# Block pairs of a fused matmul and rotary embedding, cut into two half-row tiles with mirrored weights

## The chip, the cores and the metric

The kernel runs on one core of a Trainium2 chip. The time is the device time of one execution in microseconds, as the profiler and the timer see it, and the kernels compared read the same inputs. Five engines work side by side: TensorE (PE, whose weight loads are listed apart as PEld), VectorE (DVE), ScalarE (ACT), GpSimd (POOL) and SyncE (SP). SyncE computes nothing and only issues transfers. Sixteen DMA engines move data between HBM and SBUF.

## The reference

The inputs are x (16 batches of 512 rows of 768 numbers), a weight of 768 x 768, and cos and sin of 512 x 64, all float32.

```
y = np.matmul(x, weight)                      # 8192 x 768 rows in all
y = y.reshape(batch, seq, 12, 64)
y1, y2 = y[..., :32], y[..., 32:]
out1 = y1 * cos1 - y2 * sin1                  # cos, sin by position in the sequence,
out2 = y2 * cos2 + y1 * sin2                  # the same for all heads and batches
out = np.concatenate([out1, out2], axis=-1)
```

## The kernel before, in words

The 8192 rows are cut into 64 tiles of 128 rows, and four tiles make a group, so there are 16 groups, g = 0 to 15. A group's result is 4 x 768 = 3072 columns of float32, which fill six of the eight PSUM banks: the tensor `py`. Two tiles make a pair, `(g, 0)` and `(g, 1)`; a pair owns three of the six banks.

TensorE contracts over partitions, so every tile of x must stand with its 768 inner numbers on partitions. There are two ways to that. An **ordinary tile** is loaded by SP as 128 rows of 3 KB into `xs` (`load`, L205), rounded to float16 by ACT into `xc` (`cast`), turned by TensorE through the identity into the PSUM tile `pt` (`turn_rows`, L266, twelve matmuls of 64 columns), and brought back to SBUF as `xt` by ACT. A **block pair** does without TensorE: four "quarters" of 32 partitions each are loaded so that each quarter holds a part of the inner dimension (`load_quarter`, L220), and one VectorE instruction turns 32 x 32 blocks for both tiles of the pair at once into `xp` (`turn_pair`, L294). Of the ten block pairs of the kernel before, `(g, 1)` for g = 5 to 14, the five with odd g are loaded in float32 by SP into `xb` and rounded by ACT into `xd` (`cast_pair`); the five with even g are loaded by a GpSimd DMA that rounds on the way, into `xh`.

The weight comes in six loads of 128 rows of 3 KB (`load_w`, L227), one for each of six chunks (t, e) of the inner dimension: inner number 6p + 2t + e stands on partition p. VectorE rounds each chunk to float16 as it comes (`cast_w`, `w_sb`). The first group starts with the chunks as they land (`mm0`, L334). From group 1 to 14 the matmuls are cut into two row halves: `walk` yields, for partitions 0 to 63 (r = 0) and 64 to 127 (r = 1), matmuls of 64 rows by 128 columns against 512 or 256 weight columns, and `both` interleaves the two streams so that the upper one is 1024 columns ahead of the lower (`LAG`). The two halves of a result add up in PSUM: one half opens a bank, and the other half closes it behind a wait on the PE's own counter (`one`, L359, `closed`).

When a bank is closed, VectorE multiplies it by cos and by sin into a product buffer (`rope`, L411, 1024 or 2048 products in one instruction), GpSimd adds the two products into the output tile `ov` (L428, one instruction of 1536 elements for a pair), and a DMA stores two tiles at a time (L449, 768 KB). There are three product buffers for groups 1 to 14, and one of them is the memory of the raw weight.

The order of the work is fixed when the program is written out. `do` records every instruction on its engine's queue with the semaphore waits that its buffers need; each engine runs its queue in order. The loop over tiles i = 4 to 63 emits matmuls for the tile, then `bturns` (the VectorE block turns, four tiles ahead), `turns` (about three ahead), `casts` (about five ahead), the GpSimd loads, and the stores. SP's loads stand in the list `fetch`; `pump` issues them as far as the ten `xs` and three `xb` buffers allow. The SP list begins with tiles 0 and 1 and weight chunk 0, tile 2 and chunks 1 and 2, tile 3 and chunks 3, 4 and 5, then cos, sin and tile 4.

Of the kernel before, what the change touches and what calls it, by code (L numbers as in the profile page):

```python
# [10 lines left out]
FP32 = mybir.dt.float32  # L11
FP16 = mybir.dt.float16
# [93 lines left out]
def kernel(  # L106
# [11 lines left out]
    f = Flow(nc, tc)  # L118
    do = f.do
    P = nc.NUM_PARTITIONS  # L120

    B, S, H = x.shape
# [3 lines left out]
    R = 32  # L126
# [3 lines left out]
    QB = 4  # L130
# [4 lines left out]


    BLOCKS = {}
    for g in range(5, 15):
        BLOCKS[g, 1] = "pool" if g % 2 == 0 and g >= 4 else "sp"

    def sbuf(name, shape, dt):
        return nc.alloc_sbuf_tensor(name, shape, dt).ap()

    NX, NB, NBH, NC, NCP, NXT, NXP, NOV = 10, 3, 3, 5, 2, 8, 4, 4

    ident = sbuf("ident", [P, P], FP16)
    cold = sbuf("cold", [P, 512], FP16)
# [6 lines left out]
    xh_b = [sbuf(f"xh{i}", [P, 2 * H], FP16) for i in range(NBH)]  # L154
# [23 lines left out]
    def ring(name, n, state={}):  # L178
        k = state.get((id(f), name), 0)
        state[id(f), name] = k + 1  # L180
        return k % n

    def copy(e, o, i_):
        return lambda eng: (
            eng.copy(out=o, in_=i_) if e == "act" else eng.tensor_copy(out=o, in_=i_)  # L185
        )

    def where(i):
        g, s = divmod(i, QB)
        return QB * (g // SB) + s, g % SB  # L190

    def pair_of(i):
        return i // QB, (i % QB) // 2
# [13 lines left out]
            writes=[f"xs{k}"], dma=f"xs{k}")  # L207

    def load_quarter(gh, q):
        g, h = gh  # L210
        b, r = where(g * QB + 2 * h)
        e = BLOCKS[gh]
        src = x[b : b + 2].rearrange("b (j a r) (q k) -> r q a (b j) k", r=SB, a=R, q=NQ)
        if q == 0:
            xs[gh] = ring("xh", NBH) if e == "pool" else ring("xb", NB)
        k = xs[gh]
        name = f"xh{k}" if e == "pool" else f"xb{k}"
        buf = xh_b[k] if e == "pool" else xb_b[k]
        dst = buf.rearrange("p (j k) -> p j k", j=2 * NQ)
        do(e, lambda eng: eng.dma_start(out=dst[ts(q, R)], in_=src[r, q]),  # L220
           writes=[f"{name}q{q}"], dma=name)

    wv = weight.rearrange("(p t e) n -> t e p n", t=NT, e=2)

    def load_w(c, e="sp"):
        t, h = c
# [9 lines left out]
    def cast(i, e):  # L236
        k = xs[i]
        c = ring("xc", NC)
        xc[i] = c
        do(e, copy(e, xc_b[c].rearrange("p (t m e) -> p t m e", t=NT, e=2),  # L240
                   xs_b[k].rearrange("p (m t e) -> p t m e", t=NT, e=2)),
           reads=[f"xs{k}"], writes=[f"xc{c}"])

    def turn(i, e):
# [29 lines left out]
    def cast_pair(gh, e="act"):  # L274
        k = xs[gh]
        c = ring("xd", NCP)
        xc[gh] = c
        do(e, copy(e, xd_b[c].rearrange("p (t j e) -> p t j e", t=NT, e=2),
                   xb_b[k].rearrange("p (j t e) -> p t j e", t=NT, e=2)),
           reads=[f"xb{k}q{q}" for q in range(NQ)], writes=[f"xd{c}"])  # L280

    def turn_pair(gh):
        g, h = gh
        z = ring("xp", NXP)
        dst = xp_b[z].bitcast(FP32)
        if BLOCKS[gh] == "pool":
            k = xs[gh]
            src = xh_b[k].bitcast(FP32).rearrange("p (j t) -> p t j", t=NT)
            rd = [f"xh{k}q{q}" for q in range(NQ)]
        else:  # L290
            c = xc[gh]
            src, rd = xd_b[c].bitcast(FP32), [f"xd{c}"]
        v = xp_b[z].rearrange("p (t m e) -> p t e m", t=NT, e=2)
        do("dve", lambda eng: eng.transpose(out=dst, in_=src), reads=rd, writes=[f"xp{z}"])  # L294
        for s in (0, 1):
            xT[g * QB + 2 * h + s] = (
                lambda t, e, s=s: v[:, t, e, ts(s, P)], f"xp{z}")

    def units(g):
        if g < LAST:
# [37 lines left out]

    def walk(pair, r):

        g, h = divmod(pair, 2)
        for bank in ((0, 1, 2) if r == 0 else (2, 0, 1)):
            opens = (r == 0) == (bank < 2)
            lo = h * 1536 + bank * 512
            parts = [(lo, lo + 512)] if bank != 1 else [(lo, lo + 256), (lo + 256, lo + 512)]
            for a, z in parts:
                i = g * QB + a // H
                for c in CHUNKS:  # L350
                    yield z - a, (g, i, a, z, r, c, opens,
                                  opens and (a, c) == (lo, CHUNKS[0]),
                                  c == CHUNKS[-1], z == lo + 512)

    def one(g, i, a, z, r, c, opens, start, ends, whole):
        s, rows, (t, h), bank = i % QB, ts(r, HP), c, a // 512
        get, key = xT[i]
        after = closed[g, bank] if not opens and c == CHUNKS[0] else 0
        do("pe", lambda eng: eng.matmul(  # L359
            py[:, a:z], get(t, h)[rows], w_sb[rows, t, h, a - s * H : z - s * H],  # L360
            start=start, stop=not opens and ends and whole, skip_group_check=True),
            reads=[key, f"w{t}{h}"], writes=[f"ps{bank}"], tick=ends, after=after)
        if ends and whole and opens:
            closed[g, bank] = f.count["pe"]
        if ends and whole and not opens:
            ready.setdefault(g, set()).add(bank)

    ready, roped = {}, set()
# [100 lines left out]


    fetch, quarters = [], []
    soon = [p for p in sorted(BLOCKS) if BLOCKS[p] == "sp"]
    for i in range(QB, NTILE):
        if soon and i >= max(2, soon[0][0] - 1) * QB:
            quarters += [(soon[0], q) for q in (0, 2, 1, 3)]
# [83 lines left out]
    pump()  # L559

    rows_on = [False]
    state = {"cast": 4, "turn": 4, "bturn": 0, "pool": 0}
    pairs = sorted(BLOCKS)
    pool_pairs = [p for p in pairs if BLOCKS[p] == "pool"]

    def casts(upto, most=NTILE):
        while state["cast"] < min(upto, NTILE) and most > 0:
            most -= 1
            i = state["cast"]
            state["cast"] += 1  # L570
            if not is_block(i):
                castx(i, "act")
            elif i % 2 == 0 and BLOCKS[pair_of(i)] == "sp":
                cast_pair(pair_of(i))
                xb_used[0] += 1
            pump()
# [14 lines left out]
            turn_pair(gh)  # L591
            state["bturn"] += 1

    def pool_loads(upto):
        while state["pool"] < len(pool_pairs):
            gh = pool_pairs[state["pool"]]
            if gh[0] * QB + 2 * gh[1] >= upto:
                return
            for q in (0, 2, 1, 3):
                load_quarter(gh, q)  # L600
            state["pool"] += 1

    stores = {}
    for g in range(LAST):
        for h in (0, 2):
# [9 lines left out]
                q = q[:3] + ("sp",)  # L615
            stores.setdefault(i, []).append(q)

    C_AHEAD, T_AHEAD, B_AHEAD, P_AHEAD = 5, 3, 4, 20

    for i in (0, 1):  # L620
        mm0(i, CHUNKS[5])
# [15 lines left out]
    for i in range(QB, NTILE):  # L637
        g, s = divmod(i, QB)
        us = units(g)
        done_to = (s + 1) * H  # L640
        rows_on[0] = QB <= i < QB * LAST - 1
        if g < LAST:
            if s % 2 == 0:
                for r in range(2):
                    lines[r].extend(walk(i // 2, r))
            for n in range(1, 4):
                both((i - QB) * 4608 + n * 1536)
                if n == 1 and i > QB:
# [66 lines left out]
```

## Time and profile before

The time before is 152.34 us, the median of three runs (152.06 to 155.32). The profiled execution took 151.85 us.

| | |
|---|---|
| profiled execution | 151.85 us, of it 150.1 us from first to last instruction |
| PE busy | 140.7 us, 94% |
| DVE busy | 126.9 us, 85% |
| POOL busy | 123.0 us, 82% |
| ACT busy | 77.9 us, 52% |
| HBM read and written | 27.79 MB and 25.17 MB, 353 GB/s over the span |
| mean granted TensorE clock | 0.986 |

Busy time is the time in which at least one instruction of the engine ran; matmuls overlap, so a busy PE need not be a PE at its peak. A group line gives the line of the kernel, the engine, the operation, the tiles as out<-in, the shapes and the count; then the busy time, the mean duration of one in ns, and the idle time of the engine just before them with what ended it. In an answer on order in time, the first number is the start and the second the duration in microseconds from the start of the span.

### The profile page before, as it was taken

How to read it: one execution, taken by the hardware profiler on the slowest of the kernel's cores; microseconds unless marked ns; L12 is line 12 of the kernel's file. 1: busy time of each engine (PE TensorE's matmuls, PEld its weight loads, DVE VectorE, ACT ScalarE, POOL GpSimd, SP SyncE). 2: the span in 40 equal slices, each digit the busy share in tenths (PEclk: the TensorE clock that was granted, in tenths of full speed). 3: DMA queues.
4: the chain of work that ended last, by engine and by line, in shares of the span. 5: the costliest groups of instructions: out<-in, count | busy, mean ns of one | idle time of the engine just before them, and what ended most of it. 6: DMA issues, size and time to landing. Idle time of an engine off the chain costs nothing.

```text
span 150.1 us, 4381 instructions
## 1 busy us (share of the span) xinstructions
PE 140.7 (94%) x1938; PEld 101.4 (68%) x1938; DVE 126.9 (85%) x92; ACT 77.9 (52%) x92; POOL 123.0 (82%) x68
## 2 busy tenths in 40 slices
PE   6879999999999999999999999999999999999930
PEld 2445567777787777777777777777777777776620
DVE  0245989887888899999999998999989998999990
ACT  3453888787777924456262905293327626264000
POOL 1000495999989988999999999999996979999990
PEclk9999999999999999999999999999999999999995
DMA  4999999999999999999999999999999999966574
GB/s 125 393 391 398 404 401 390 274 404 275 319 367 327 347 354 361 285 397 332 359 346 392 355 332 359 370 391 319 356 367 412 415 406 399 385 269 235 217 296 144
DMA packets 27556, 51.27 MB, mean 342 GB/s; under 512 B 7185, under 2 KB 13073, under 8 KB 27537
## 3 DMA queue, kind: packets, MB, share of 16 engines
q1 hardware_dynamic: 14592, 27.92, 53.8%
q10 hardware_dynamic: 7504, 21.10, 35.5%
q0 software_dynamic: 5440, 1.97, 10.6%
q8 instruction: 15, 0.25, 0.6%
q14 instruction: 5, 0.03, 0.1%
HBM read 27.79 MB, written 25.17 MB: 353 GB/s over the span
## 4 chain that ended last, share of the span: by engine, by line
PE 87%; DMA 4%; DVE 4%; SPq 1%; issue 1%; ACT 1%; DVEq 0%
PE py L359 73%; PE py L334 8%; PE pt L266 4%; DMA w_raw<-in_weight_dram 4%; DVE tq L411 2%; PE pt L251 1%; DVE ov L428 1%; SPq L205 1%; SPq L227 1%; ACT xt L185 1%; DVE xs L411 0%; DVE w_sb L185 0%; SPq L710 0%; DVEq L57 0%; SPq L116 0%
## 5 line engine op out<-in xcount | busy, mean ns | idle before, releaser
L428 POOL TENSOR_TENSOR ov<-tq 128x1536 f32<-128x1536 f32 (+3 forms) x30 | 76.3, 2564 | 18.9 <-DVE tq L411 18.8
L359 PE MATMUL py<-w_sb,xt 64*128 64x256 f16 (+1 forms) x864 | 80.7, 323 | 0.0
L411 DVE TENSOR_TENSOR tq<-py,csn 128x1024 f32<-128x1024 f32 (+2 forms) x46 | 74.8, 1656 | 5.4 <-PE py L359 5.0
L359 PEld LDWEIGHTS py<-w_sb,xt 64*128 64x128 f16 x864 | 53.2, 94 | 17.8 <-DVE tq L411 0.4
L185 ACT COPY xt<-pt 128x768 f16<-128x768 f16 x42 | 33.6, 801 | 47.8 <-PE pt L266 43.5
L359 PE MATMUL py<-w_sb,xp 64*128 64x256 f16 (+1 forms) x480 | 46.8, 323 | 0.0
L185 ACT CAST xc<-xs 128x768 f16<-128x768 f32 x44 | 39.1, 909 | 12.1 <-DMA xs<-in_x_dram 12.0
L411 DVE TENSOR_TENSOR w_raw<-py,csn 128x1024 f32<-128x1024 f32 (+1 forms) x21 | 35.2, 1676 | 4.4 <-PE py L359 4.2
L428 POOL TENSOR_TENSOR ov<-w_raw 128x1536 f32<-128x1536 f32 (+1 forms) x12 | 35.0, 2926 | 3.6 <-DVE w_raw L411 3.4
L359 PEld LDWEIGHTS py<-w_sb,xp 64*128 64x128 f16 x480 | 30.4, 94 | 9.5
L334 PE MATMUL py<-w_sb,xt 128*128 128x256 f16 (+1 forms) x90 | 15.7, 323 | 1.3 <-DVE w_sb L185 1.1
L266 PEld LDWEIGHTS pt<-ident,xc 64*128 64x128 f16 x432 | 14.1, 95 | 1.9 <-ACT xt L185 0.6
L334 PEld LDWEIGHTS py<-w_sb,xt 128*128 128x128 f16 x90 | 8.1, 98 | 7.2 <-DVE w_sb L185 2.7
L266 PE MATMUL pt<-ident,xc 64*128 64x64 f16 x432 | 12.3, 190 | 0.3 <-ACT xt L185 0.3
L220 POOL DMA_DIRECT2D xh<-in_x_dram x20 | 11.7, 590 | 0.0
L185 ACT CAST xd<-xb 128x1536 f16<-128x1536 f32 x5 | 8.2, 1637 | 0.0
L294 DVE STREAM_TRANSPOSE xp<-xh 128x768 f32<-128x768 f32 x5 | 6.2, 1241 | 0.0
L510 PE MATMUL py<-cold 128*128 128x512 f16 x12 | 4.8, 569 | 1.4 <-DVE cold L453 1.4
L185 DVE CAST w_sb<-w_raw 128x768 f16<-128x768 f32 x6 | 3.3, 558 | 3.3 <-DMA w_raw<-in_weight_dram 3.3
L185 DVE COPY xt<-pt 128x768 f16<-128x768 f16 x2 | 1.1, 558 | 5.2 <-PE pt L251 5.2
L294 DVE STREAM_TRANSPOSE xp<-xd 128x768 f32<-128x768 f32 x5 | 4.8, 969 | 0.0
L251 PEld LDWEIGHTS pt<-ident,xc 128*128 128x128 f16 x48 | 3.2, 104 | 2.1 <-ACT xc L185 1.3
(16 smaller groups left out, 14.5 us busy)
## 6 DMA issues: line engine op xcount, KB each, us to landing
out_dram<-ov ACTq DMA_DIRECT2D x26, 768.0 KB, 8.8
xs<-in_x_dram SPq DMA_DIRECT2D x44, 384.0 KB, 17.3
xb<-in_x_dram SPq DMA_DIRECT2D x20, 192.0 KB, 17.4
out_dram<-ov SPq DMA_DIRECT2D x4, 768.0 KB, 3.7
w_raw<-in_weight_dram SPq DMA_DIRECT2D x6, 384.0 KB, 6.9
xh<-in_x_dram POOLq DMA_DIRECT2D x20, 96.0 KB, 12.8
out_dram<-ov SPq DMA_DIRECT2D x1, 384.0 KB, 2.3
out_dram<-ov ACTq DMA_DIRECT2D x1, 384.0 KB, 2.3
```

The lines of the kernel that those rows point to most:

```text
L185: eng.copy(out=o, in_=i_) if e == "act" else eng.tensor_copy(out=o, in_=i_)
L205: do(e, lambda eng: eng.dma_start(out=xs_b[k], in_=x[b].rearrange("(p r) h -> r p h", r=SB)[r]), writes=[f"xs{k}"], dma=f"xs{k}")
L220: do(e, lambda eng: eng.dma_start(out=dst[ts(q, R)], in_=src[r, q]), writes=[f"{name}q{q}"], dma=name)
L227: do(e, lambda eng: eng.dma_start(out=w_raw[:, t, h], in_=wv[t, h]), writes=[f"wr{t}{h}"], dma=f"w{t}{h}")
L251: do("pe", lambda eng: eng.transpose(pt[:, t, h, :], src[:, t, h, :], ident), reads=[f"xc{c}", "ident"], writes=[f"pt{k}"], tick=(t, h) == ...
L266: do("pe", lambda eng: eng.transpose(pts[r][:, t, h, :], src[rows, t, h, :], ident[rows, rows]), reads=[f"xc{c}", "ident"], writes=[f"pt{r ...
L294: do("dve", lambda eng: eng.transpose(out=dst, in_=src), reads=rd, writes=[f"xp{z}"])
L334: do("pe", lambda eng: eng.matmul(ps, get(t, h), w_sb[:, t, h, a - s * H : z - s * H], start=start, stop=stop), reads=[key, f"w{t}{h}"], w ...
L359: do("pe", lambda eng: eng.matmul(py[:, a:z], get(t, h)[rows], w_sb[rows, t, h, a - s * H : z - s * H], start=start, stop=not opens and en ...
L411: do("dve", lambda eng: eng.tensor_tensor(out=tq.rearrange("p j (h d) -> p j h d", d=D), in0=ps.rearrange("p (h d) -> p h d", d=D) .unsque ...
L428: do(adder, lambda eng: eng.tensor_tensor(out=ov_b[o][:, ds(c0, w)].rearrange("p (h t d) -> p h t d", t=2, d=HD), in0=tq[:, 0].rearrange(" ...
L510: do("pe", lambda eng: eng.matmul(py[:, ts(b, 512)], cold[:, 0:P], cold, start=True, stop=warmed[0] < WARM - 6), reads=["cold"], writes=[f ...
```

## The change

The block pairs become `(g, 1)` for g = 2 to 14, thirteen in place of ten, and all are loaded in float32 and rounded by ACT. Each quarter now holds half of the inner dimension of one tile: quarters 0 and 1 (partitions 0 to 63) hold the first tile of the pair, quarters 2 and 3 (partitions 64 to 127) the second. A quarter is 32 partitions by four runs of 384 numbers, 1536 bytes each. The GpSimd loads and the `xh` buffers are gone, and there are four `xb` buffers. SP loads quarters 0 and 1 of each pair; ACT issues quarters 2 and 3, ten and nine tiles ahead (only the first pair is loaded by SP alone).

As each half of the partitions now carries a whole tile, the upper row half must meet all 768 inner numbers, and so must the lower. The weight's inner numbers are laid out anew for that, as 12m + 6u + 2t + e on partition 64u + m, and a second weight tensor `w_un` holds the two halves exchanged: six VectorE copies of 64 partitions by 1536 float16 numbers (`mirror`), emitted after tiles 5 to 10. The copies on VectorE's queue stand one behind each of the six multiplications of pairs (1,0), (1,1) and (2,0); the block turn of pair (2,1) stands between the 512-column multiplication of (1,1) and its copy.

For a block pair `walk` gives the upper half the columns 0 to 768 and the lower half 768 to 1536. The first and third bank each belong to one half alone ("only"); of the middle bank the lower half opens its part first, and the upper half closes it. The matmuls of a block pair stay 48 in number, with the same widths.

In the program, a weight load now reads its source as 2 x 64 rows (u, m) of 768 numbers, and not as 128 rows; its destination is 128 rows as before.

```diff
-    for g in range(5, 15):
-        BLOCKS[g, 1] = "pool" if g % 2 == 0 and g >= 4 else "sp"
+    for g in range(2, 15):
+        BLOCKS[g, 1] = "act" if BLOCKS else "sp"
...
+    w_un = sbuf("w_un", [P, NT, 2, H], FP16)
...
         g, h = gh
-        b, r = where(g * QB + 2 * h)
-        e = BLOCKS[gh]
-        src = x[b : b + 2].rearrange("b (j a r) (q k) -> r q a (b j) k", r=SB, a=R, q=NQ)
...
+        b, r = where(g * QB + 2 * h + q // 2)
+        src = x[b].rearrange("(j a r) (q k) -> r q a j k", r=SB, a=R, q=2)[r, q % 2]
+        k = xs[gh] = sorted(BLOCKS).index(gh) % NB
+        e = BLOCKS[gh] if q > 1 else "sp"
...
-    wv = weight.rearrange("(p t e) n -> t e p n", t=NT, e=2)
+    wv = weight.rearrange("(m u t e) n -> t e u m n", u=2, t=NT, e=2)
...
+    def mirror(u, t):
+
+        do("dve", lambda eng: eng.tensor_copy(
+            out=w_un[ts(1 - u, HP), t], in_=w_sb[ts(u, HP), t]),
+            reads=[f"w{t}{h}" for h in (0, 1)], writes=[f"v{u}{t}"])
...
+        if gh in BLOCKS:
+            plan = ([("only", [(0, 512)]), ("close", [(512, 768)])] if r == 0 else
+                    [("open", [(768, 1024)]), ("only", [(1024, 1536)])])
...
+                    for t in range(2 * NT):
+                        own = (t < NT) == (r == 0)
+                        u, tt = t // NT, t % NT
+                        for c in range(2):
+                            w = (w_sb if own else w_un)[rows, tt, c, n0 : n0 + cols]
...
+        if i - QB - 1 in range(6):
+            mirror((i - QB - 1) % 2, (i - QB - 1) // 2)
         casts(i + 1 + (C_AHEAD if i > QB else 4), 1 + i % 2)
-        pool_loads(i + P_AHEAD)
+        for piece in pieces_at.get(i, ()):
+            load_quarter(*piece)
```

More of the change, by code (lines that the diff above doesn't have):

```diff
@@ L137 @@
     BLOCKS = {}
-    for g in range(5, 15):
-        BLOCKS[g, 1] = "pool" if g % 2 == 0 and g >= 4 else "sp"
+    for g in range(2, 15):
+        BLOCKS[g, 1] = "act" if BLOCKS else "sp"
     def sbuf(name, shape, dt):
         return nc.alloc_sbuf_tensor(name, shape, dt).ap()
-    NX, NB, NBH, NC, NCP, NXT, NXP, NOV = 10, 3, 3, 5, 2, 8, 4, 4
+    NX, NB, NC, NCP, NXT, NXP, NOV = 10, 4, 5, 2, 8, 4, 4
     ident = sbuf("ident", [P, P], FP16)
@@ L151 @@
     w_sb = sbuf("w_sb", [P, NT, 2, H], FP16)
+    w_un = sbuf("w_un", [P, NT, 2, H], FP16)
     xs_b = [sbuf(f"xs{i}", [P, H], FP32) for i in range(NX)]
     xb_b = [sbuf(f"xb{i}", [P, 2 * H], FP32) for i in range(NB)]
-    xh_b = [sbuf(f"xh{i}", [P, 2 * H], FP16) for i in range(NBH)]
     xc_b = [sbuf(f"xc{i}", [P, H], FP16) for i in range(NC)]
@@ L210, in load_quarter @@
         g, h = gh
-        b, r = where(g * QB + 2 * h)
-        e = BLOCKS[gh]
-        src = x[b : b + 2].rearrange("b (j a r) (q k) -> r q a (b j) k", r=SB, a=R, q=NQ)
[L214 to L221, printed above, removed]
-    wv = weight.rearrange("(p t e) n -> t e p n", t=NT, e=2)
+        b, r = where(g * QB + 2 * h + q // 2)
+        src = x[b].rearrange("(j a r) (q k) -> r q a j k", r=SB, a=R, q=2)[r, q % 2]
+        k = xs[gh] = sorted(BLOCKS).index(gh) % NB
+        e = BLOCKS[gh] if q > 1 else "sp"
+        dst = xb_b[k].rearrange("p (j k) -> p j k", j=4)
+        do(e, lambda eng: eng.dma_start(out=dst[ts(q, R)], in_=src),
+           writes=[f"xb{k}q{q}"], dma=f"xb{k}{e}")
+    wv = weight.rearrange("(m u t e) n -> t e u m n", u=2, t=NT, e=2)
     def load_w(c, e="sp"):
@@ L239, in cast @@
         xc[i] = c
-        do(e, copy(e, xc_b[c].rearrange("p (t m e) -> p t m e", t=NT, e=2),
-                   xs_b[k].rearrange("p (m t e) -> p t m e", t=NT, e=2)),
+        do(e, copy(e, xc_b[c].rearrange("p (t u m e) -> p t u m e", t=NT, u=2, e=2),
+                   xs_b[k].rearrange("p (m u t e) -> p t u m e", t=NT, u=2, e=2)),
            reads=[f"xs{k}"], writes=[f"xc{c}"])
@@ L277, in cast_pair @@
         xc[gh] = c
-        do(e, copy(e, xd_b[c].rearrange("p (t j e) -> p t j e", t=NT, e=2),
-                   xb_b[k].rearrange("p (j t e) -> p t j e", t=NT, e=2)),
+        do(e, copy(e, xd_b[c].rearrange("p (t j e) -> p t j e", t=2 * NT, e=2),
+                   xb_b[k].rearrange("p (j t e) -> p t j e", t=2 * NT, e=2)),
            reads=[f"xb{k}q{q}" for q in range(NQ)], writes=[f"xd{c}"])
@@ L285, in turn_pair @@
         dst = xp_b[z].bitcast(FP32)
[L286 to L293, printed above, removed]
-        do("dve", lambda eng: eng.transpose(out=dst, in_=src), reads=rd, writes=[f"xp{z}"])
-        for s in (0, 1):
-            xT[g * QB + 2 * h + s] = (
-                lambda t, e, s=s: v[:, t, e, ts(s, P)], f"xp{z}")
+        c = xc[gh]
+        src, rd = xd_b[c].bitcast(FP32), [f"xd{c}"]
+        v = xp_b[z].rearrange("p (t m e) -> p t e m", t=2 * NT, e=2)
+        do("dve", lambda eng: eng.transpose(out=dst, in_=src), reads=rd, writes=[f"xp{z}"])
+        xT[gh] = v, f"xp{z}"
+    def mirror(u, t):
+        do("dve", lambda eng: eng.tensor_copy(
+            out=w_un[ts(1 - u, HP), t], in_=w_sb[ts(u, HP), t]),
+            reads=[f"w{t}{h}" for h in (0, 1)], writes=[f"v{u}{t}"])
     def units(g):
@@ L341, in walk @@
     def walk(pair, r):
[L343 to L347, printed above, removed]
-            for a, z in parts:
[L349 to L358, printed above, removed]
+        g, h = gh = divmod(pair, 2)
+        i, lo, rows = pair * 2, h * 1536, ts(r, HP)
+        if gh in BLOCKS:
+            plan = ([("only", [(0, 512)]), ("close", [(512, 768)])] if r == 0 else
+                    [("open", [(768, 1024)]), ("only", [(1024, 1536)])])
+        else:
+            wide = [[(0, 512)], [(512, 768), (768, 1024)], [(1024, 1536)]]
+            plan = [("close" if (k == 2) == (r == 0) else "open", wide[k])
+                    for k in ((0, 1, 2) if r == 0 else (2, 0, 1))]
@@ new lines, in walk @@
+        for mode, parts in plan:
+            for a, z in parts:
+                s, cols, bank = a // H, z - a, (lo + a) // 512
+                n0 = a - s * H
+                if gh in BLOCKS:
+                    v, key = xT[gh]
+                    todo = []
+                    for t in range(2 * NT):
[3 more added lines that the diff above has]
+                            w = (w_sb if own else w_un)[rows, tt, c, n0 : n0 + cols]
+                            wk = f"w{tt}{c}" if own else f"v{1 - r}{tt}"
+                            todo.append((v[rows, t, c, :], w, [key, wk]))
+                else:
+                    get, key = xT[i + s]
+                    todo = [(get(t, c)[rows], w_sb[rows, t, c, n0 : n0 + cols], [key, f"w{t}{c}"])
+                            for t, c in CHUNKS]
+                for n, (x_, w_, keys) in enumerate(todo):
+                    begin, end = n == 0, n == len(todo) - 1
+                    yield cols, (g, bank, py[:, lo + a : lo + z], x_, w_, keys,
+                                 mode != "close" and begin and (a, z) == parts[0],
+                                 mode == "close" and begin,
+                                 end, end and (a, z) == parts[-1], mode)
@@ L359, in one @@
+    def one(g, bank, ps, x_, w_, keys, start, handed, ends, last, mode):
+        after = closed[g, bank] if handed else 0
         do("pe", lambda eng: eng.matmul(
[L360 to L363, printed above, removed]
+            ps, x_, w_, start=start, stop=mode != "open" and last, skip_group_check=True),
+            reads=keys, writes=[f"ps{bank}"], tick=ends, after=after)
+        if last and mode == "open":
@@ L364, in one @@
             closed[g, bank] = f.count["pe"]
-        if ends and whole and not opens:
+        elif last:
             ready.setdefault(g, set()).add(bank)
@@ L471 @@
     fetch, quarters = [], []
-    soon = [p for p in sorted(BLOCKS) if BLOCKS[p] == "sp"]
+    soon = sorted(BLOCKS)
     for i in range(QB, NTILE):
-        if soon and i >= max(2, soon[0][0] - 1) * QB:
-            quarters += [(soon[0], q) for q in (0, 2, 1, 3)]
+        if soon and i >= soon[0][0] * QB + 2 * soon[0][1] - 4:
+            quarters += [(soon[0], q) for q in range(NQ) if q < 2 or BLOCKS[soon[0]] == "sp"]
             soon.pop(0)
@@ L561 @@
     rows_on = [False]
-    state = {"cast": 4, "turn": 4, "bturn": 0, "pool": 0}
+    state = {"cast": 4, "turn": 4, "bturn": 0}
     pairs = sorted(BLOCKS)
-    pool_pairs = [p for p in pairs if BLOCKS[p] == "pool"]
     def casts(upto, most=NTILE):
@@ L572, in casts @@
                 castx(i, "act")
-            elif i % 2 == 0 and BLOCKS[pair_of(i)] == "sp":
+            elif i % 2 == 0:
                 cast_pair(pair_of(i))
@@ L592, in bturns @@
             state["bturn"] += 1
[L594 to L601, printed above, removed]
     stores = {}
@@ L616 @@
             stores.setdefault(i, []).append(q)
-    C_AHEAD, T_AHEAD, B_AHEAD, P_AHEAD = 5, 3, 4, 20
+    pieces_at = {}
+    for n, (g, h) in enumerate(pairs):
+        if BLOCKS[g, h] == "act":
+            for q, lead in ((2, 10), (3, 9)):
+                pieces_at.setdefault(g * QB + 2 * h - lead, []).append(((g, h), q))
+    C_AHEAD, T_AHEAD, B_AHEAD = 5, 3, 4
     for i in (0, 1):
```

## The prediction

> **What bounds the kernel now.** I read the shares of busy time first, then the chain that ended last, and then the stretches around each edit. The page's first part and the chain's shares:
>
> ```profile
> PE 140.7 (94%) x1938; PEld 101.4 (68%) x1938; DVE 126.9 (85%) x92; ACT 77.9 (52%) x92; POOL 123.0 (82%) x68
> ...
> PE 87%; DMA 4%; DVE 4%; SPq 1%; issue 1%; ACT 1%; DVEq 0%
> ```
>
> TensorE carries 87% of the chain. The chain in order of time shows one ordinary group's second pair and one block pair (start, duration, what):
>
> ```profile
> 57.07 1.95 PE py L359 x18
> 59.02 0.18 PE pt L266 x10
> 59.20 5.85 PE py L359 x56
> 65.05 0.17 PE pt L266 x12
> ```
>
> A tile's matmuls take 1.95 us, an ordinary tile's turn 0.175 us, and a block pair has no turn: 5.85 us are three tiles in one piece. From 21.6 us to 141 us PE waits for nobody. A tile has 6 x 768 columns, so PE passes 4608 / 1.95 = 2363 columns per us in each row half.
>
> Before that stands the start. VectorE's row in order of time, where it rounds the last weight chunks, and the group of the weight loads:
>
> ```profile
> 11.70 0.56 DVE L185 CAST w_sb<-w_raw 128x768 f16<-128x768 f32 x1 [1.40 <-DMA w_raw<-in_weight_dram]
> 12.68 0.56 DVE L185 CAST w_sb<-w_raw 128x768 f16<-128x768 f32 x1 [0.42 <-DMA w_raw<-in_weight_dram]
> 13.66 0.56 DVE L185 CAST w_sb<-w_raw 128x768 f16<-128x768 f32 x1 [0.43 <-DMA w_raw<-in_weight_dram]
> ...
> w_raw<-in_weight_dram SPq DMA_DIRECT2D x6, 384.0 KB, 6.9
> ```
>
> Each chunk is rounded as it lands, 0.98 us apart: a load of 384 KB passes in 0.98 us. The table of stretches (busy time by engine, granted clock, DMA share, GB/s) says on how many engines:
>
> ```profile
> 10.00:15.00 5.00, 4.87 (x35) 2.63 (x34) 2.43 (x6) 1.84 (x3) 0.00 (x0) 1.00 1.04 403
> ...
> 145.00:150.10 5.10, 0.00 (x0) 0.00 (x0) 1.60 (x2) 0.00 (x0) 1.31 (x2) 0.58 0.53 187
> ```
>
> With SP's loads alone in flight all sixteen DMA engines are busy (share 1.04). So one engine passes 128 / 16 = 8 rows of 3 KB in 0.98 us, 0.1225 us a row. The second row shows the TensorE clock falling (0.58) once PE rests.
>
> **Block pairs, the part on the path.** Three pairs more, six tiles, lose their turns: 6 x 0.175 = -1.05 us. The 48 matmuls of a pair keep their widths and so their 3.9 us; the upper half closes the middle bank 2048 columns after the lower has opened it, so that wait (0.87 us of room) costs nothing. Nothing else can make the kernel faster, since PE is the chain.
>
> **Parts beside the path.** POOL loses twenty issues of 590 ns (11.7 us), but its adds already wait for VectorE (18.8 us), so 0. ACT loses six evictions of 801 ns and six casts of 909 ns and gains eight pair casts of 1637 ns: +2.8 us; its 47.8 us of waiting for PE hide them, and without that cover they would be 0.35 us a pair. It also issues 24 quarters, 0.38 to 0.43 us each like its stores: 0.8 us a group against 3.5 us of idle in a group. VectorE trades five turns of 1241 and five of 969 ns for thirteen of 969: +1.6 us over thirteen groups, in which it sits at 7.6 to 7.9 of 8.15 us today; the even groups get lighter, so 0. SP issues two quarters a pair in place of four, and four pairs may be ahead: no queue is longer in the first microseconds, since the x tiles up to 6 come first.
>
> A late quarter is the open wait here. ACT issues the last one right after it rounded the previous pair, so 8.15 - 1.64 = 6.5 us before it wants it. ACT's stores take 8.8 us (median) to land, but the store in front of the quarter is by then 5.6 us old, so I expect some 4 us and no wait. Behind the waiting cast stand an eviction and the next casts; about 4 us of lateness are covered (2.1 us until VectorE's turn in the trace, 1.9 us of bank room).
>
> **The mirror copies.** A copy of 1536 float16 numbers isn't in the trace. The nearest row, the rounding of 768 numbers in 0.56 us, has some 0.155 us fixed, so 0.96 us at its rate and 0.56 us at twice it. The lower half of pair (2,1) wants the copies early: the fifth copy 0.86 us into the pair, and the upper half wants the sixth after 5120 columns and one turn, 2.34 us in. Count from 22.39 us, where VectorE starts on pair (1,0) in the trace. It starts a new 512-column multiplication after 1.14 us, a 1024-column one after 2.17, a block turn after 0.89 (52.25 to 53.39 to 54.28, 62.67 to 64.84). With copies of 0.56 us the queue runs: 1.14, copy 1.70, 3.87, copy 4.43, 5.57, turn 6.46, copy 7.02, 9.19, copy 9.75, 10.89, fifth copy 11.45, 13.62, sixth copy 14.18. Pair (2,1) starts 3 x 4.25 - 3.3 = 9.45 us after that point, so PE wants the fifth at 10.31 and has it at 11.54 (stall 1.23), and wants the sixth at 13.02 and has it at 14.27 (1.25): **2.5 us**. With 0.96 us the same count gives 4.9.
>
> POOL may make it longer. The one place where VectorE reads SBUF twice beside a POOL add is the end:
>
> ```profile
> 143.56 1.28 DVE L411 TENSOR_TENSOR xs<-pt,csn 128x512 f32<-128x512 f32 x2
> 144.76 1.84 DVE L428 TENSOR_TENSOR ov<-xs 128x256 f32<-128x256 f32 x2
> ```
>
> 512 elements take 0.68 us, so 256 should take 0.41, and took 0.92 to 0.98. If a copy is held likewise until a running add (3.47 us) ends, the copies behind the three 512-column multiplications wait 0.9, 1.4 and 2.3 us: +4.7, so 7.2 or 9.6 us; if the other copies lose to an add as well, 14. I take **6.0**, the middle of 2.5 and 9.6, and keep 0 to 14. [...]
>
> **The weight loads, the largest term.** Each of the six now reads 2 x 64 rows. Every transfer of the trace has 128 or 32 as its outermost count, which sixteen divides. If the work of a transfer is dealt out along its outermost dimension, two engines get 64 rows each: 64 x 0.1225 = 7.84 us a load in place of 0.98, and six times 6.86 = **+41.2 us**. If it is dealt out by rows whatever their nesting, 0. No row stands in between. I take the first: the even split over sixteen is seen only where the outermost count allows it, and the source of the new loads alone can't be cut in sixteen there. Tile 4 and all later loads stand behind the weights on those two engines, so nothing runs ahead. [...]
>
> The last chunk is then rounded at 14.22 + 41.2 = 55.4 us. PE still owes 9 x 768 columns and two turns, 3.7 us at full clock, but has been idle in most of each 7.84 us. After a rest its clock is low: at the start the first nine 512-column matmuls took 4.02 us, 0.45 each, against 512 / 2363 = 0.22 later. With half speed for the first 4.5 us (as at the start) that is 4.5 + 1.45 = 5.9 us; today PE goes from 14.22 to 18.11 us, 3.9. So **+1.9** (0 if it stays warm, 3.5 if cold throughout).
>
> **Sum**, against the profiled execution (150.1 us span, 1.75 us around it, 151.85; the median of the runs is 0.5 us higher): 151.85 + 41.2 + 1.9 - 1.05 + 6.0 = **199.9 us**. With the ends of the copies and the clock 192 to 209.5; a little room below for a faster row makes 191 to 210.
>
> **Rivals.**
> - *The loads spread over sixteen engines as before.* Then 151.85 - 1.05 + the copies: 153.3 with 2.5 us, 156.8 with 6.0, 150.8 if they hide. This is the other side: from 4.1 us of copies on it is slower by over 2%, below that not. Already with eight engines six loads would cost 6 x 0.98 = 5.9 us, so only sixteen leads here. For it: a load is 128 rows of 3 KB either way, to the same 128 partitions. Against it: the outermost count. Chance 0.13, split evenly at 2%, with 0.01 for faster by more.
> - *Two engines, and late quarters too.* If the last quarter needs 12.6 us as ACT's slowest store, the cast is 6.1 us late, 2.1 beyond its cover, in twelve groups: 25 us, 225 in all. For it: ACT's queue carries 1.9 MB a group, 0.4 more than today. Against it: DMA engines lose the small GpSimd packets. Chance 0.05.
> - *The forecast*: 0.82.
>
> So faster 0.01, within 2% (about what a measurement here tells from no change) 0.06, slower 0.93. The range leaves out both rivals.
>
> **What would show it.** The roundings of w_sb 7.8 to 8.8 us apart and the last near 55 us; the DMA share near 2/16 until then; PE's steady stretch beginning near 61 us; 8.15 us for groups 2 to 14; PE waits for DVE w_un in pair (2,1) of some 6 us in all. A last rounding near 14 us would prove the main step wrong; a PE wait for ACT in each group would point to the quarters.

## The result, and the profile after

The changed kernel takes 204.71 us (median of four runs, 204.35 to 206.18) where the kernel before takes 153.11 in the same comparison (152.06 to 155.32): 1.342 times as long, 95% interval 1.336 to 1.349. The ratio is formed from the fast executions of both kernels alone, and the kernel before has slower ones among its four. The profiled execution took 204.82 us, with a span of 203.0. The page's first part and the shares of the chain, as they stand after the change:

```profile
PE 150.3 (74%) x1866; PEld 105.8 (52%) x1866; DVE 135.8 (67%) x101; ACT 78.5 (39%) x88; POOL 112.8 (56%) x48
...
PE 57%; DMA 17%; DVE 11%; SPq 11%; issue 1%; ACT 0%; DVEq 0%
```

TensorE falls from 87% of the chain to 57%. What came in is DMA and SP's queue, 28% together, and VectorE with 11%. The first two are the start, in which the weights come late, as VectorE's row in order of time shows (start, duration, what, and the idle time before it with its releaser):

```profile
13.51 0.56 DVE L185 CAST w_sb<-w_raw 128x768 f16<-128x768 f32 x1 [5.65 <-DMA w_raw<-in_weight_dram]
22.44 0.56 DVE L185 CAST w_sb<-w_raw 128x768 f16<-128x768 f32 x1 [8.37 <-DMA w_raw<-in_weight_dram]
30.09 0.56 DVE L185 CAST w_sb<-w_raw 128x768 f16<-128x768 f32 x1 [7.08 <-DMA w_raw<-in_weight_dram]
...
46.51 0.56 DVE L185 CAST w_sb<-w_raw 128x768 f16<-128x768 f32 x1 [7.25 <-DMA w_raw<-in_weight_dram]
58.00 0.56 DVE L185 CAST w_sb<-w_raw 128x768 f16<-128x768 f32 x1 [10.93 <-DMA w_raw<-in_weight_dram]
```

The chunks come 7.6 to 8.9 us apart and the last one 11.5 us after its neighbour; the last rounding starts at 58.00 us instead of 13.66. The stretches of the start and one of the body (duration, busy time of PE, PEld, DVE, ACT and POOL, then the granted clock, the DMA share and GB/s):

```profile
31.00:43.00 12.00, 5.37 (x22) 2.43 (x20) 0.56 (x1) 1.66 (x2) 0.00 (x0) 0.64 0.13 51
43.00:58.00 15.00, 2.10 (x6) 0.73 (x6) 0.56 (x2) 0.00 (x0) 0.00 (x0) 0.50 0.85 234
58.00:65.00 7.00, 6.39 (x30) 3.49 (x30) 5.57 (x6) 2.63 (x4) 3.36 (x2) 0.54 0.98 263
84.87:88.28 3.41, 3.29 (x30) 1.71 (x27) 2.50 (x2) 1.34 (x2) 1.39 (x1) 0.50 1.07 220
```

While only a weight load is in flight the DMA share is 0.13, which is two engines of sixteen, and they carry 51 GB/s. From 43 us on later loads run beside the last weights. When the weights are in, TensorE works at half its clock (0.54 from 58 to 65 us).

The time can be split at the last rounding and at the start of the two row halves (`walk`, L359 before, L373 after), since the chain passes through both:

| stretch | before | after | difference |
|---|---|---|---|
| start of span to the last rounding of w_sb | 13.66 | 58.00 | +44.34 |
| last rounding to the first matmul of the row halves | 4.45 | 7.13 | +2.68 |
| that matmul to VectorE's part of the end | 123.11 | 129.15 | +6.04 |
| the end, and what lies around the span | 10.63 | 10.54 | -0.09 |
| profiled execution | 151.85 | 204.82 | +52.97 |

The third stretch holds the mirror copies. VectorE's copies, then GpSimd's adds, then TensorE's waits in the same answers in order of time:

```profile
73.58 0.56 DVE L291 COPY w_un<-w_sb 64x1536 f16<-64x1536 f16 x1
76.31 1.56 DVE L291 COPY w_un<-w_sb 64x1536 f16<-64x1536 f16 x1
80.23 0.56 DVE L291 COPY w_un<-w_sb 64x1536 f16<-64x1536 f16 x1
82.07 2.42 DVE L291 COPY w_un<-w_sb 64x1536 f16<-64x1536 f16 x1
...
73.63 3.82 POOL L441 TENSOR_TENSOR ov<-w_raw 128x1536 f32<-128x1536 f32 x1 [3.66 <-DVE w_raw L424]
80.28 3.79 POOL L441 TENSOR_TENSOR ov<-tq 128x1536 f32<-128x1536 f32 x1 [2.82 <-DVE tq L424]
...
80.25 0.28 PE L373 MATMUL py<-w_un,xp 64*128 64x256 f16 x1 [1.03 <-DVE tq L424]
84.54 0.28 PE L373 MATMUL py<-w_un,xp 64*128 64x256 f16 x1 [3.68 <-DVE w_un L291]
```

The two long copies end at 77.87 and 84.49 us, each 0.42 us after the add that ran beside it (73.63 + 3.82 and 80.28 + 3.79). PE waits 4.71 us in pair (2,1), and then runs at half clock from 84.87 to 88.28 us, as the last row of the stretches shows, which loses 1.7 us of work (half of 3.41). Together that is 6.4 of the 7.1 us that remain when the 1.05 us of the saved turns are added back to 6.04; 0.7 us are not assigned.

After that PE waits for nobody, and a group takes 8.15 us, from 95.95 to 104.10 us for example (chain in order of time):

```profile
95.95 5.84 PE py L373 x55
101.98 1.94 PE py L373 x19
104.10 5.84 PE py L373 x55
```

### The profile page after: what moved, and what is told of

The parts are those of the page before. It is cut to its first block, busy times and chain, and to the rows that moved or that the text cites. A ratio compares the mean times of both kernels' runs of the same rounds, so it can differ in the third digit from the quotient of the medians.

```text
span 203.0 us, 4263 instructions
## 1 busy us (share of the span) xinstructions
PE 150.3 (74%) x1866; PEld 105.8 (52%) x1866; DVE 135.8 (67%) x101; ACT 78.5 (39%) x88; POOL 112.8 (56%) x48
## 4 chain that ended last, share of the span: by engine, by line
PE 57%; DMA 17%; DVE 11%; SPq 11%; issue 1%; ACT 0%; DVEq 0%
PE py L373 49%; DMA w_raw<-in_weight_dram 17%; SPq L224 7%; PE py L328 5%; DVE tq L424 5%; SPq L205 4%; DVE w_un L291 3%; PE pt L263 3%; DVE w_raw L424 2%; PE pt L248 1%; DVE ov L441 1%; DVE xp L286 0%; ACT xt L185 0%; DVE xs L424 0%; DVE w_sb L185 0%
## 5 line engine op out<-in xcount | busy, mean ns | idle before, releaser
L373 PE MATMUL py<-w_sb,xt 64*128 64x256 f16 (+1 forms) x720 | 69.2, 323 | 0.0
L373 PEld LDWEIGHTS py<-w_sb,xt 64*128 64x128 f16 x720 | 46.3, 94 | 16.0 <-issue 0.7
L373 PE MATMUL py<-w_un,xp 64*128 64x512 f16 (+1 forms) x312 | 49.8, 330 | 4.8 <-DVE w_un L291 3.7
L328 PE MATMUL py<-w_sb,xt 128*128 128x256 f16 (+1 forms) x90 | 23.2, 419 | 40.0 <-DVE w_sb L185 40.0
L185 ACT CAST xc<-xs 128x768 f16<-128x768 f32 x38 | 32.4, 894 | 50.6 <-DMA xs<-in_x_dram 50.6
L373 PE MATMUL py<-w_sb,xp 64*128 64x512 f16 (+1 forms) x312 | 50.4, 325 | 0.0
L373 PEld LDWEIGHTS py<-w_un,xp 64*128 64x128 f16 x312 | 24.9, 95 | 9.1 <-DVE w_un L291 4.6
L373 PEld LDWEIGHTS py<-w_sb,xp 64*128 64x128 f16 x312 | 26.2, 95 | 5.7 <-issue 0.6
L185 ACT CAST xd<-xb 128x1536 f16<-128x1536 f32 x13 | 20.7, 1595 | 0.0
L286 DVE STREAM_TRANSPOSE xp<-xd 128x768 f32<-128x768 f32 x13 | 12.6, 969 | 0.0
L291 DVE COPY w_un<-w_sb 64x1536 f16<-64x1536 f16 x6 | 6.2, 1033 | 0.2
```

The lines of the kernel that those rows point to most:

```text
L291: do("dve", lambda eng: eng.tensor_copy(out=w_un[ts(1 - u, HP), t], in_=w_sb[ts(u, HP), t]), reads=[f"w{t}{h}" for h in (0, 1)], writes=[f ...
L328: do("pe", lambda eng: eng.matmul(ps, get(t, h), w_sb[:, t, h, a - s * H : z - s * H], start=start, stop=stop), reads=[key, f"w{t}{h}"], w ...
L373: do("pe", lambda eng: eng.matmul(ps, x_, w_, start=start, stop=mode != "open" and last, skip_group_check=True), reads=keys, writes=[f"ps{ ...
```

## Experiments: the form of the weight load

**Undo the load's form in the changed kernel (e1).** Everything else of the change stays.

```diff
-        do(e, lambda eng: eng.dma_start(out=w_raw[:, t, h], in_=wv[t, h]),
-           writes=[f"wr{t}{h}"], dma=f"w{t}{h}")
+        for u in range(2):
+            do(e, lambda eng, u=u: eng.dma_start(out=w_raw[ts(u, HP), t, h], in_=wv[t, h, u]),
+               writes=[f"wr{t}{h}" + "b" * u], dma=f"w{t}{h}")
...
```

> The changed kernel with each weight load given out as two DMAs of 64 rows (partitions 0 to 63, then 64 to 127); the layout of the weight in SBUF, the mirror copies, the block pairs and their quarters stay. Theory (a load whose source has 2 as its outermost count runs on two DMA engines, and that is the main cost): last rounding of w_sb near 14 us in place of 58.0, and the 2.7 us of cold TensorE clock go too, so 204.8 - 44.3 - 2.7 = 157.8 us; taken as 156 to 160. Rival (the form of the load doesn't matter, the weights are late because something else, the quarters or tile loads, shares their queues): about 204 us.

Measured: 164.67 us, 1.083 times before (1.080 to 1.086). Of the 52 us, 40 are gone, so the form of the load is the main cause. But 7 us more than expected remain, and 5.2 in the profiled execution (163.04 against 157.8). Its last rounding is at 17.46 us, not at 14, which is 3.8 of these. Some 1.2 lie in the body: pair (2,1) costs 4.9 us of waiting (3.7 for a copy, 1.2 behind VectorE) in place of 4.7, and TensorE then works 5.4 us at half clock in place of 3.4, which loses 1.0 us more. Why the other executions take 1.1 to 2.0 us more than the profiled one stays open.

**Do the load's form alone, in the kernel before,** with three outermost counts: u=2 as below (e2), and u=4 (e3) and u=16 (e4) in the same line.

```diff
-    wv = weight.rearrange("(p t e) n -> t e p n", t=NT, e=2)
+    wv = weight.rearrange("(m u t e) n -> t e u m n", u=2, t=NT, e=2)
```

> The kernel before with nothing changed but the source of the six weight loads, which is read as 2 x 64 rows as in the changed kernel. The rows of the weight then stand on other partitions than x's inner numbers, so the result isn't the reference's; the amount of work is the same. Theory (two engines): loads 7.8 us apart, the last landing near 56 to 58 us, 152 + 44 + 3 = 199 us (195 to 203). Rival (the late weights come from the rest of the change, its quarters, copies or queues): 152 us.

> As the run with 2 x 64 rows, but the source is read as 4 x 32 rows; again the weight rows stand on other partitions, so the result isn't the reference's. Theory (the outermost count is the number of engines): four engines, 32 rows x 0.1225 = 3.9 us a load, six times 3.9 - 0.98 = 17.6 us later, and 1 to 3 us of cold clock: 170 to 173 us. Rival (a source that can't be joined into one run of 128 rows costs per row or falls to one slow path): as with 2 x 64 rows, 195 to 203 us.

> As the run with 2 x 64 rows, but the source is read as 16 x 8 rows, which can't be joined into 128 rows either; the result isn't the reference's for the same reason. Theory (the outermost count is the number of engines): sixteen engines, 0.98 us a load, 152 us. Rival (the nesting itself is slow, whatever the count): 195 to 203 us.

Measured: 197.66 us with u = 2, 177.65 with u = 4 and 156.4 with u = 16, against 152.25. One stretch of each, in this order, in which no more than one load at a time is in flight for u = 2 and 4 (columns as above), from three kernels:

```profile
8.00:16.00 8.00, 1.60 (x7) 0.65 (x8) 0.56 (x1) 0.88 (x1) 0.00 (x0) 0.68 0.13 52
```

```profile
14.00:20.00 6.00, 1.46 (x4) 0.43 (x4) 1.05 (x2) 0.69 (x1) 0.00 (x0) 0.50 0.26 103
```

```profile
8.00:16.00 8.00, 4.47 (x30) 2.11 (x30) 2.03 (x4) 3.17 (x4) 0.00 (x0) 1.00 1.04 252
```

The DMA shares are 2/16, 4/16 and 16/16: in these three runs the number of engines is the outermost count, and no other nested count was run. With 3 KB rows, 52 GB/s on two engines are 0.118 us a row and 103 GB/s on four 0.119, so a lone engine is as fast as the prediction took it (0.1225).

Two of the sizes missed, and both misses teach something. With u = 4 the time should have been 170 to 173. VectorE's last roundings of that kernel show why:

```profile
15.69 0.56 DVE L185 CAST w_sb<-w_raw 128x768 f16<-128x768 f32 x1 [3.98 <-DMA w_raw<-in_weight_dram]
19.51 0.56 DVE L185 CAST w_sb<-w_raw 128x768 f16<-128x768 f32 x1 [3.26 <-DMA w_raw<-in_weight_dram]
24.55 0.56 DVE L185 CAST w_sb<-w_raw 128x768 f16<-128x768 f32 x1 [4.48 <-DMA w_raw<-in_weight_dram]
30.80 0.56 DVE L185 CAST w_sb<-w_raw 128x768 f16<-128x768 f32 x1 [5.69 <-DMA w_raw<-in_weight_dram]
36.81 0.56 DVE L185 CAST w_sb<-w_raw 128x768 f16<-128x768 f32 x1 [5.45 <-DMA w_raw<-in_weight_dram]
```

The third chunk came 3.82 us after the second, as four engines should make it, but the last two take 6.25 and 6.0 us: tile loads are in flight by then (DMA share 0.80 from 22 to 24 us, against 0.26 from 14 to 20), and the weight takes longer. It is the same with the last load of the changed kernel, 11.5 us in place of 7.8. With u = 16 the engines are all at work and still move 252 GB/s where the kernel before has 404 in its stretch of 8 to 10 us, so a row takes 0.195 us. A DMA share of 1.0 isn't yet a full rate.

**What makes the two loads of 64 rows slow (e9).** The kernel before with each chunk as two loads of 64 rows, in its own row order:

```diff
-    wv = weight.rearrange("(p t e) n -> t e p n", t=NT, e=2)
+    wv = weight.rearrange("(u m t e) n -> t e u m n", u=2, t=NT, e=2)
...
-        do(e, lambda eng: eng.dma_start(out=w_raw[:, t, h], in_=wv[t, h]),
+        for u in range(2):
+            do(e, lambda eng, u=u: eng.dma_start(out=w_raw[ts(u, HP), t, h], in_=wv[t, h, u]),
...
```

> The kernel before, with each weight load given out as two DMAs of 64 rows to partitions 0 to 63 and 64 to 127, in the row order of the kernel before (partition p holds inner number 6p + 2t + e, so that the source rows are 18 KB apart as they were). It asks why a chunk took 1.6 us in e1 in place of 0.98, with all sixteen engines busy. If a load to 64 partitions alone is slow, a chunk again takes 1.6 us, the last rounding is near 17.4 us, and the time is 152.2 + 3.7 = 156 us. If it was the doubled row distance of the source (36 KB), a chunk takes 0.98 to 1.1 us and the time is 152 to 153 us.

Measured: 156.12 us, 1.025 times before (1.019 to 1.032); the last rounding at 18.24 us; its stretch:

```profile
8.00:16.00 8.00, 4.68 (x31) 2.22 (x32) 2.13 (x4) 3.34 (x4) 0.00 (x0) 1.00 1.05 256
```

So the doubled row distance is not what made the chunks of the first experiment slow; loads to 64 partitions are slow in both row orders tried. Nor is it a fixed cost of each small load: among the trace's DMA packets of that stretch, a single row of 3 KB takes 0.205 us (median), against 0.121 us in the kernel before between 8 and 14 us. The run with u = 16 writes all 128 partitions in each load and is as slow (252 GB/s against 256 here), so that writing half of the partitions is not shown to be the reason either, and no run here tells what is.

**Both halves at once,** from two queues (e12, on top of e11, with ten block pairs and early copies, of which the next section tells):

```diff
-            do(e, lambda eng, u=u: eng.dma_start(out=w_raw[ts(u, HP), t, h], in_=wv[t, h, u]),
+            do(("sp", "act")[u], lambda eng, u=u: eng.dma_start(out=w_raw[ts(u, HP), t, h], in_=wv[t, h, u]),
...
```

> As e11 (ten block pairs, early copies, two DMAs of 64 rows for a chunk), with the loads to partitions 64 to 127 issued by ACT, so that both halves of a chunk can be under way at the same time. It asks what makes a load to 64 partitions slow. If one half of the partitions takes less than the sixteen engines give, two halves at once are as fast as one load of 128 rows: 0.98 us a chunk, the last rounding near 14 us in place of 18 to 19, and 158.9 - 4 = 155 us. If each small DMA costs its time by itself (rows of 0.2 us whatever is beside them), chunks stay 1.6 us apart and the time is that of e11, 157 to 159 us. Tiles 0 and 1 may land up to 1 us later, since ACT's loads are beside them.

Measured: 160.41 us, 1.055 times before (1.052 to 1.058), slower than either case expected. Its stretch of 8 to 10 us, in which the halves from both queues are in flight:

```profile
8.00:10.00 2.00, 1.84 (x9) 0.71 (x7) 0.56 (x2) 0.86 (x1) 0.00 (x0) 1.00 1.05 270
```

Two halves side by side don't add up to one whole: from 6 to 18 us they move 259 GB/s, as the 256 of e9 with one queue from 8 to 16 us. The last rounding is at 20.09 us, and PE waits 2.7 us at the start for tiles that now share the engines with ACT's loads. The case in which two halves at once are as fast as one whole load did not come.

## Experiments: the copies, and what the late weights had covered

**The weight as before, the rest of the change kept (e5).** The quarters pay for it with two DMAs each, in runs of 768 bytes.

```diff
-        src = x[b].rearrange("(j a r) (q k) -> r q a j k", r=SB, a=R, q=2)[r, q % 2]
+        src = x[b].rearrange("(j a r) (u q k) -> r q u a j k", r=SB, a=R, u=2, q=2)[r, q % 2]
...
-    wv = weight.rearrange("(m u t e) n -> t e u m n", u=2, t=NT, e=2)
+    wv = weight.rearrange("(p t e) n -> t e p n", t=NT, e=2)
...
```

> The changed kernel with the weight laid out and loaded as in the kernel before (inner number 6p + 2t + e on partition p, 128 rows in one DMA). To fit, each quarter holds inner numbers of two runs of 192 and is given out as two DMAs; block pairs, their matmuls and the late mirror copies stay. Theory (of the 10.8 us that the run with two DMAs of 64 rows lies over the kernel before, 3.7 come from its weights landing later, the rest from the copies): the weights are in at 13.7 us, 163.0 - 3.7 = 159.3 us (158 to 161), PE waits of about 5 us for the copies in pair (2,1). Rival (the weights' 3.7 us are covered by the copies' wait, so nothing is won): 163 us.

Measured: 164.17 us, 1.079 times before (1.073 to 1.084). The weights are in at 14.3 us, and nothing is won against the first experiment. It is not quite what the rival said either: PE waits 4.5 us for VectorE and its copies as before, and 4.7 us more for ordinary tiles that ACT brings late.

**The copies early (e6, on top of e5).** Four between the roundings, two behind 1024-column multiplications.

```diff
+    mirror(0, 0)
+    mirror(1, 0)
...
         cast_w(c, "dve")
+        mirror(CHUNKS.index(c) - 3, 1)
...
-        if i - QB - 1 in range(6):
-            mirror((i - QB - 1) % 2, (i - QB - 1) // 2)
+        if i in {6: (0, 2), 8: (1, 2)}:
+            mirror(*{6: (0, 2), 8: (1, 2)}[i])
```

> As e5, but four of the six mirror copies are emitted between the roundings of the weight chunks, before GpSimd has its first add, and the last two behind the multiplications of 1024 columns of pairs (1,0) and (1,1). Theory (the copies cost only because they were behind 512-column multiplications beside a running GpSimd add, and too late for pair (2,1)): every copy takes 0.56 us, PE waits for none, and the time is 151.85 - 1.05 + some 0.2 = 151.0 us (150.3 to 152.5). Rival (six copies of 0.56 us delay VectorE by 3.4 us wherever they stand): 154 us or more.

Measured: 1.057 times before (1.051 to 1.062), 160.8 us by the ratio, and far from 151.0. The part on the copies held: each takes 0.56 to 0.57 us and PE waits for none. But PE now waits 8.0 us in the body for tiles and for the first block turns, which come late because their loads do.

**Three copies behind 512 (e7) or behind 1024 columns (e8),** three early in both kernels. The tile behind which a copy is emitted decides; first the edit of e6 for 512 columns, then the one for 1024:

```diff
-        if i in {6: (0, 2), 8: (1, 2)}:
+        if i in {5: (1, 1), 7: (0, 2), 9: (1, 2)}:
...
```

```diff
-        if i in {6: (0, 2), 8: (1, 2)}:
+        if i in {6: (1, 1), 8: (0, 2), 10: (1, 2)}:
...
```

> As e6, but only three copies early; the other three stand each behind a multiplication of 512 columns, of pairs (1,0), (1,1) and (2,0), where the change puts its odd copies. Theory (a copy and a GpSimd add exclude each other for a whole instruction): these three last until the running add has ended, some 1.2, 1.6 and up to 2.4 us, in place of 0.56. Rival (a copy's time depends on its rows or on TensorE's reading of the weight, not on GpSimd): the same three durations as in e8.

> As e7, but the three late copies stand behind the multiplications of 1024 columns of the same pairs, where GpSimd is about to start an add and runs none. Theory (exclusion): 0.56 us each, and the adds of these pairs are stretched from 3.47 to some 3.8 us. Rival (not GpSimd): the same durations as in e7.

Copies and adds in order of time, first of the kernel with the copies behind 512 columns, then of the other:

```profile
24.95 0.56 DVE L292 COPY w_un<-w_sb 64x1536 f16<-64x1536 f16 x1
30.73 1.33 DVE L292 COPY w_un<-w_sb 64x1536 f16<-64x1536 f16 x1
35.55 2.79 DVE L292 COPY w_un<-w_sb 64x1536 f16<-64x1536 f16 x1
...
28.19 3.46 POOL L442 TENSOR_TENSOR ov<-w_raw 128x1536 f32<-128x1536 f32 x1 [3.45 <-DVE w_raw L425]
34.47 3.45 POOL L442 TENSOR_TENSOR ov<-tq 128x1536 f32<-128x1536 f32 x1 [2.82 <-DVE tq L425]
```

```profile
29.34 0.56 DVE L292 COPY w_un<-w_sb 64x1536 f16<-64x1536 f16 x1
34.70 0.56 DVE L292 COPY w_un<-w_sb 64x1536 f16<-64x1536 f16 x1
38.74 0.56 DVE L292 COPY w_un<-w_sb 64x1536 f16<-64x1536 f16 x1
...
29.39 3.83 POOL L442 TENSOR_TENSOR ov<-w_raw 128x1536 f32<-128x1536 f32 x1 [4.32 <-DVE w_raw L425]
34.74 3.83 POOL L442 TENSOR_TENSOR ov<-tq 128x1536 f32<-128x1536 f32 x1 [1.52 <-DVE tq L425]
```

The same copy takes 0.56 us where GpSimd is idle or is just about to start, and where an add is running it ends 0.41 to 0.42 us after that add (30.73 + 1.33 = 32.06 against 28.19 + 3.46 = 31.65; 38.34 against 37.92). When the copy is first, the add takes 3.83 us in place of 3.46. That agrees with exclusion by a whole instruction, from both sides; the first copy of the first kernel found GpSimd idle, which the expected 1.2 us hadn't allowed for. The times of these two (160.16 and 162.50 us, one execution each) say nothing on the copies, since both wait for tiles.

**What makes the tiles late.** Back to the first experiment's loads, whose quarters have runs of 1536 bytes, with early copies (e10); then the same with ten block pairs (e11), for which one line more changes:

```diff
-    for g in range(2, 15):
+    for g in range(5, 15):
```

> As e1 (two DMAs of 64 rows for a chunk, quarters in runs of 1536 bytes as the change has them), with the mirror copies early and unblocked as in e6. It asks whether e6 stayed 8 us above its 151.0 because its quarters are in runs of 768 bytes, or because thirteen block pairs that begin in group 2 need more of the DMA engines in the first 40 us than these can give once nothing else is late. Runs of 768 bytes to blame: PE waits for no tile, 163.0 - 4.9 - some 2 of cold clock = 156 us. Pairs that begin too early to blame: PE waits for tiles by ACT some 3 to 7 us in all between 20 and 110 us, and the time is 159 to 162 us.

> As e10, with ten block pairs, groups 5 to 14, as in the kernel before. Three turned pairs are 6 x 0.175 us of TensorE more, so 1.05 us more than e10 if PE is the bound in both: 157 us. If the early pairs make tiles late in e10, this one is faster than e10: 151.85 + 3.7 for the weights = 155.5 us.

Measured: 1.079 times before with thirteen pairs (1.072 to 1.086; 163.93 us) and 1.040 with ten (1.032 to 1.048; 158.5 us by the ratio). PE's waits with thirteen pairs, and one early stretch with thirteen and with ten:

```profile
PE py L374 <- ACT xt L185: 3.2, 5, 1.3
PE pt L264 <- ACT xt L185: 2.4, 2, 1.4
PE py L374 <- DVE xp L287: 1.3, 1, 1.3
```

```profile
24.00:32.00 8.00, 5.65 (x98) 3.90 (x93) 4.73 (x4) 4.88 (x8) 5.05 (x3) 1.00 1.05 248
```

```profile
24.00:32.00 8.00, 7.74 (x130) 5.49 (x130) 6.88 (x5) 7.06 (x11) 6.00 (x4) 1.00 1.03 401
```

Runs of 768 bytes are not the main reason, since PE waits nearly as long with runs of 1536 bytes (6.9 us in place of 8.0). Pairs that begin in group 2 are: with thirteen pairs, quarters, each to 32 partitions, stand among the tiles there, and the engines are full (share 1.05) but move 248 GB/s; with ten pairs, the first of which stands in group 5, they move 401 at a share of 1.03. A row of 3 KB takes 0.211 us (median of the DMA packets) with thirteen pairs and 0.125 with ten. What in a quarter slows the others isn't shown; between 80 and 100 us, with quarters and stores under way, the kernel with thirteen pairs moves 404 GB/s. Without the three early pairs the kernel is some 6 us faster by the two ratios, though it turns six tiles more. The kernel with ten is still 2 to 3 us above 152 + 3.7; what these are stays open. No kernel tried here beats the kernel before.

## Why the prediction was right, point by point

The prediction, 199.9 us with 191 to 210, named the cause and its mechanism, and the range held 204.7. By its steps:

- **Weight loads, +41.2 us: +44.34.** Two engines is shown, by the share of 0.13 and by the three counts. The time of a row was right where a load is alone (0.118 us against 0.1225). What was missed is the last load: the prediction let all later loads wait behind the weights "so nothing runs ahead". Until 43 us that came out: SP's issues of the last three weight loads and of cos lasted from 18.33 to 42.99 us, so the later loads weren't given out before. From then on they run on all the engines beside the last weights (DMA share 0.85), and the last one took 11.5 us for 7.8. That is 3.6 us, more than the whole difference.
- **Cold clock, +1.9 us: +2.68.** The mechanism held (granted clock 0.54 from 58 to 65 us); half speed lasted nearly the whole stretch and not 4.5 us of it. At the start, from which the prediction took the half speed, the 0.45 us a matmul stood beside a granted clock of 1.00 (1.4 to 5.9 us, kernel before); the low clock after a rest is shown by this stretch and by the 0.50 of the one ahead of it (43 to 58 us).
- **Three more pairs, -1.05 us.** Held in this kernel, 8.15 us a group from group 2 on, with PE waiting for nobody after 87.45 us. It held because of its cover: the weights were 44 us late, so the tiles and quarters had come in by then. With the weights in at 18.4 us and the copies early, the same three pairs cost some 6 us; with the weights in at 17.5 us but the copies late (e1), PE waits only 0.6 us for tiles, since it stands 4.9 us for the copies in any case.
- **Mirror copies, +6.0 us: +7.1.** A copy takes 0.56 us alone, so the faster of the two assumed rates, and an add holds it up, as the count with 7.2 us supposed. That count agrees only in its sum, which is luck: it had 7.2 us of waiting, and there were 4.71, and 1.7 from a clock that fell to half after the longest wait, a term that the prediction had only at the start. Of the six copies two were held long, not three, since GpSimd was idle at the first. With three late copies (e7, e8) whichever of a copy and an add started first held the other up: a copy took 0.56 us ahead of an add and up to 2.79 beside a running one, an add 3.46 us with a copy waiting behind it and 3.83 with a copy just ahead of it. The 0.155 us of fixed time behind both assumed rates is an estimate; rows of the kernel before, 0.228 us for 128 numbers and 0.558 for 768, give 0.16.
- **Parts beside the path, 0.** The ACT quarters were never waited for: they land in 7.6 us (median), more than the 4 expected, and the cover was not used up. The rival of late quarters (225 us) didn't occur.
- **The rival of sixteen engines, 150.8 to 156.8 us,** would have been priced wrong. The kernel that comes nearest to it, with the weight loaded as before and the quarters in shorter runs, takes 164.2 us: the rival lacked the tiles that come late once the weights don't (4.7 us of PE's waiting) and the half clock after the copies' wait.

## What to carry to other kernels

Before a load is given a nested source, look at its outermost count and at the partitions that it writes: six loads with an outermost count of 2 cost 44 us here, and the same rows as halves to 64 partitions still 3.7. A part that is free beside a long stall must be priced again without that stall: three block pairs saved 1 us in this kernel, and cost 6 when the weights came at 18 us and the copies held nothing up. Place a VectorE copy where GpSimd is idle or about to start, since the same copy takes 0.56 us there and up to 2.8 us beside a running add.

## What was not expected of the hardware

All sixteen DMA engines can be busy (share 1.04 to 1.05) and move 250 GB/s or 404, by the form of the loads alone (u = 16 against the kernel before). TensorE's granted clock fell to 0.50 for 3.41 us in the middle of the body after waits of 1.03 and 3.68 us close together, so that they cost 1.7 us more than their length. A load on two engines took half as long again when loads on all engines ran beside it (11.5 us in place of 7.8).
